# The last chunk of a down projection in two token parts: 192 tokens first, then 128

## The chip, the cores and the metric

The kernel runs on one core of a Trainium2 chip. A core has a matrix engine (TensorE, PE in the profile; PEld is its loading of weights, which stands beside PE), a vector engine (DVE), a scalar engine (ACT), GpSimd (POOL), and SyncE (SP), which here only issues transfers; ACT issues transfers too. Sixteen DMA engines carry the transfers. Matrix products are written to PSUM (eight banks of 128 x 512 float32); everything else lies in SBUF. The metric is the device time of one execution in microseconds (us); lower is better.

## The reference, cut to what matters

One step of a one-layer decoder on 320 tokens (256 of a prompt, 64 of eight running sequences), width 2048. The part that matters here is the last one:

```python
def rms_norm(x, w):
    y = xf * lax.rsqrt(jnp.mean(xf * xf, axis=-1, keepdims=True) + EPS)
    return y * w

f, _ = conv_ffn(rms_norm(x, p["norm_ffn_pre"]), ...)   # ... (gelu(g) * u) @ w_down
x = x + rms_norm(f, p["norm_ffn_post"])                # the output y
```

`w_down` is 5632 x 2048. `f` must be whole for a token, all 2048 columns, before its root (the rsqrt of its mean square) is known; then every column of the token is multiplied by the root, `x` is added, and the result is stored.

## The kernel before, in words

Activations lie with the model dimension on the partitions: `acc[:, nb, :]` is block `nb` (128 of 2048 columns) of `f` for 320 tokens, 16 blocks in all. Every weight is read as float32 and split into two float32r parts, `hi` (ACT casts, L128) and `lo` (DVE subtracts, L130); the activations are split alike (`fhi`, `flo`). One product of 128 x 128 weights is then three matmul instructions in `accumulate` (L141 to L143), each with the weight block loaded anew and 320 columns streamed. `slab` loads 512 KB of weights at a time (SP queue, L124) into rotating buffers, three each of `wraw`, `whi` and `wlo`.

The feed-forward part goes over 11 chunks `g` of 512 inner columns: `ffn_up(g+1)` makes the next chunk, `chunk_out(..., g, ...)` (L222) multiplies chunk `g` into all 16 blocks: for each block four inner tiles times three matmuls, 12 in all, into one of four PSUM banks of pool `mm`; DVE adds the bank to `acc` (L234). In the last chunk `last(nb)` (L1145) follows each block: the block's square is added to a sum over blocks, `sq4` (ACT squares and POOL adds, L299 and L300; the last three blocks by ACT and DVE, L316 to L325), and ACT multiplies the block by its norm weights (L1148).

Then comes the tail, in an order written out by hand (`behind` and `issue_after` chain instructions on an engine):

- `token_sums` (L282): PE multiplies the squares by a column of ones and so sums them over the partitions; once for `sq4`, once for the last block's square `one`;
- `rsqrt_by_root` (L260): a few vector operations on 128 x 3 values and ACT's square root, whose table was loaded earlier by `root_table`;
- `spread` (L286): PE transposes the root back so that it lies along the tokens, in PSUM (`r4`), and for POOL in SBUF (`r4s`);
- `hand_over` (L1228): PE copies blocks of `x1` (the layer's `x`) into PSUM with an identity matrix, in plain float32, for the additions;
- blocks 0 to 3: DVE multiplies by the root (L1259), PE adds the block to `x1` in PSUM (L1269), ACT copies it out (L1270) and stores it; blocks 4 to 11: DVE multiplies and adds (L1264), SP stores; blocks 12 to 15: POOL multiplies and adds (L1276), SP stores.

The tile framework places waits and orders each engine's queue by priority; `first()` is a high priority. Engines run their queues strictly in that order.

Of the kernel before, what the change touches and what calls it, by code (L numbers as in the profile page):

```python
# [17 lines left out]
P = 128  # L18
# [16 lines left out]
def hybrid_step(  # L35
# [21 lines left out]
    def misc(name):  # L57
        return ms.tile([P, 512], F32, tag="ms", name=name)
# [56 lines left out]

    first_raw = []

    def slab(src):
        n = src.shape[2]
        with tc.high_priority(offset=100000):  # L120
            m = n * src.shape[1]
            raw = wp.tile([P, 1024], F32, tag="wraw", name="wraw", bufs=3) if len(first_raw) < 2 else first_raw.pop(0)
            with turn() if first_raw else nullcontext():
                slab_load.append(sp.dma_start(raw[:, :m].rearrange("p (a n) -> p a n", n=n), src).ins)  # L124
            if first_raw:
                in_turn.append(slab_load[-1])
            hi = wp.tile([P, 1024], F32R, tag="whi", name="whi", bufs=3)
            act.copy(hi[:, :m], raw[:, :m])  # L128
            lo = wp.tile([P, 1024], F32R, tag="wlo", name="wlo", bufs=3)
# [9 lines left out]
    def accumulate(ps, w, xhi, xlo, first, last):  # L139
        whi, wlo = w  # L140
        pe.matmul(ps, whi, xhi, start=first, stop=False)  # L141
        pe.matmul(ps, whi, xlo, start=False, stop=False)  # L142
        newest[0] = pe.matmul(ps, wlo, xhi, start=False, stop=last).ins  # L143
# [75 lines left out]
    acc = None  # L219
    pd_last = []  # L220

    def chunk_out(w, ck, hi, lo, begins, done=None, rate=1):  # L222

        for nb in range(KD):
            if nb % 2 == 0:
                wb = slab(rows_of(w, 4 * ck, 4, P * nb, 256))
            ps = mm.tile([P, 512], F32, tag="mm", name=f"pd_{ck}_{nb}")
            for k in range(4):
                made = accumulate(ps[:, :NT], wb(k, nb % 2), hi[:, k, :], lo[:, k, :], k == 0, k == 3)
            with first():  # L230
                if begins:
                    act.copy(acc[:, nb, :], ps[:, :NT])
                else:
                    dve.tensor_tensor(out=acc[:, nb, :], in0=acc[:, nb, :], in1=ps[:, :NT], op=ALU.add)  # L234
# [24 lines left out]

    def rsqrt_by_root(ps, scale):  # L260

        v, w, r, s = (tp.tile([P, 3], F32, tag=f"rq_{n}", name=f"rs_{n}", bufs=1) for n in "vwrs")
        dve.tensor_scalar(out=v, in0=ps, scalar1=scale, scalar2=EPS, op0=ALU.mult, op1=ALU.add)
# [4 lines left out]
        rsqrt_ins.append(dve.scalar_tensor_tensor(out=r, in0=v, scalar=1.5, in1=r, op0=ALU.add, op1=ALU.mult).ins)  # L268
        return r
# [4 lines left out]
        with tc.issue_after(behind):  # L274
            act.activation(there, ones[:, 0:1], AF.Sqrt)

    def token_sums(sq, ps=None, more=False):

        begins = ps is None
        ps = misc("tsum") if begins else ps  # L280
        for c, o in enumerate((0, P, NT - P)):
            ins = pe.matmul(ps[:, c:c + 1], sq[:, o:o + P], ones[:, 0:1], start=begins and c == 0, stop=not more and c == 2).ins  # L282
        sums_ins.append(ins)
        return ps if more else ps[:, 0:3]

    def spread(r, out=None):  # L286

        ps = misc("spread")
        for c, o in ((2, NT - P), (0, 0), (1, P)):
            spread_ins.append(pe.transpose(ps[:, o:o + P], r[:, c:c + 1].to_broadcast([P, P]), ident).ins)  # L290
        if out is not None:
            act.copy(out, ps[:, :NT])
        return ps[:, :NT]

    def add_square(total, x, begins, adder=pool, place=("sq", 2)):
        if begins:
# [761 lines left out]
    with tc.tile_pool(name="fp", bufs=1) as fp:  # L1058
# [81 lines left out]

        sq4 = fp.tile([P, NT], F32, name="sq4")

        squares, one = squares_of(sq4, True)

        def last(nb):  # L1145
            a = acc[:, nb, :]
            squares(nb)
            act.activation(a, a, AF.Copy, scale=col(prm_at["norm"][2] + nb))  # L1148

        def renewals():  # L1150

# [57 lines left out]
        for g in range(NG):  # L1209
            hi, lo = nxt  # L1210
            if g < NG - 1:
                nxt = ffn_up(g + 1)
            if g == 0:
                acc = fp.tile([P, KD, NT], F32, name="acc_ffn")
            if g == NG - 1:
                finish(grow)
            chunk_out(ffn_w_down, g, hi, lo, g == 0, last if g == NG - 1 else None)

        act.dma_start(o_fconv_p, ptf)


        banks, more = (mm, "mm"), (ms, "ms")
        x1p, behind = {}, {}

        def after(engine):
            return tc.issue_after(behind[engine]) if engine in behind else nullcontext()

        def hand_over(*blocks, where=banks):  # L1228
            for nb in blocks:
                x1p[nb] = where[0].tile([P, 512], F32, tag=where[1], name="x1p")[:, :NT]  # L1230
                with after(pe):
                    behind[pe] = pe.matmul(x1p[nb], ident, x1[:, nb, :], start=True, stop=nb > 3).ins

        def stored(queue, k, n):
            with after(queue):
                behind[queue] = queue.dma_start(o_y[:, k:k + n, :], acc[:, k:k + n, :]).ins

        behind[pe] = pd_last[-1]
        with after(pe):
            sums = token_sums(sq4, more=True)  # L1240
        behind[pe] = sums_ins[-1]
        hand_over(0)
        with after(pe):
            sums = token_sums(one[0], sums)
        r = rsqrt_by_root(sums, 1.0 / D)
        behind[pe] = sums_ins[-1]
        hand_over(4, 5)
        with after(pe):
            r4 = spread(r)
        behind[pe] = spread_ins[-1]  # L1250
        with after(pe):
            r4s = fp.tile([P, NT], F32, name="r4s")
            spread(r, r4s)
        behind[pe] = spread_ins[-1]

        def timed(engine, k, n, root):
            f = acc[:, k:k + n, :]
            with after(engine):
                behind[engine] = engine.tensor_tensor(out=f, in0=f, in1=root.unsqueeze(1).to_broadcast([P, n, NT]), op=ALU.mult).ins  # L1259

        def whole(k, n):
            timed(dve, k, n, r4)
            for nb in range(k, k + n):
                behind[dve] = dve.tensor_tensor(out=acc[:, nb, :], in0=acc[:, nb, :], in1=x1p[nb], op=ALU.add).ins  # L1264
            stored(sp, k, n)

        def by_pe(nb):
            with after(pe):
                behind[pe] = pe.matmul(x1p[nb], ident, acc[:, nb, :], start=False, stop=True).ins  # L1269
            act.copy(acc[:, nb, :], x1p[nb])  # L1270
            stored(act, nb, 1)

        def by_pool(k):
            timed(pool, k, 2, r4s)
            with after(pool):
                behind[pool] = pool.tensor_tensor(out=acc[:, k:k + 2, :], in0=acc[:, k:k + 2, :], in1=x1[:, k:k + 2, :], op=ALU.add).ins  # L1276
            stored(sp, k, 2)

        timed(dve, 0, 1, r4)
        hand_over(1)  # L1280
        by_pe(0)
        whole(4, 2)
        hand_over(6, 7, where=more)
        timed(dve, 1, 1, r4)
        by_pe(1)
        by_pool(12)
        whole(6, 2)
        hand_over(2, 8)
        timed(dve, 2, 1, r4)
        by_pe(2)  # L1290
        hand_over(9, 3)
        timed(dve, 3, 1, r4)
        by_pe(3)
        whole(8, 2)
        by_pool(14)
        hand_over(10, 11)
        whole(10, 1)
        whole(11, 1)


_OUTS = [
# [81 lines left out]
```

## Time and profile before

| | us |
|---|---|
| median of 3 runs | 1778.87 (1778.08 to 1780.75) |
| profiled execution | 1777.68 |
| its span, first to last instruction | 1775.6 |
| PE busy | 1765.8 (99%) |
| last product of the last chunk ends | 1759.58 |
| last vector operation ends | 1772.42 |
| last store is issued | 1772.45 |

The granted clock is full in this execution. The page gives busy times by engine and, for groups of equal instructions, line, tile names, shapes, count, total and mean duration, and what ended the idle time before. The chain of waits is followed back from the last instruction. In a timeline a row is one instruction or a run of equal ones (xN) with its start and length. `PEld` rows are weight loads, `SPq` and `ACTq` rows are transfers issued by that engine.

### The profile page before, as it was taken

The numbers are of one execution on the slowest core, as the hardware profiler recorded it, in microseconds if no ns is written. First come the engines' busy times: TensorE is split into PE (matmuls) and PEld (weight loads), VectorE is DVE, ScalarE is ACT, GpSimd is POOL, SyncE is SP. The second block draws the span as 40 slices with busy tenths as digits, with TensorE's granted clock in tenths as the row PEclk, the third lists the DMA queues.
The fourth block names the chain that finished last, engine by engine and source line by source line (L and its number), as shares of the span: only waits on it lengthen the run. The fifth ranks groups of instructions, "written<-read, shape, count | busy, mean of one in ns | idle before, by whom it ended". The sixth has DMA issues, their size and how long they took to land.

```text
span 1775.6 us, 31255 instructions
## 1 busy us (share of the span) xinstructions
PE 1765.8 (99%) x12234; PEld 1740.7 (98%) x12234; DVE 1186.2 (67%) x2055; ACT 799.4 (45%) x1108; POOL 272.7 (15%) x591
## 2 busy tenths in 40 slices
PE   9999999999999999999999999999999999999998
PEld 8999999999999999999999999999999999999998
DVE  7448854657887778577966666767666575656475
ACT  7344545333545454445645434343434343433335
POOL 1003210000211111012322212021101010101004
PEclk9999999999999999999999999999999999999999
DMA  7455654445664654545566656566564445544543
GB/s 245 143 166 167 191 155 149 151 153 185 227 207 150 201 161 145 157 162 155 161 190 198 207 173 208 181 197 205 180 192 147 153 149 152 156 145 154 151 151 106
DMA packets 228498, 303.04 MB, mean 171 GB/s; under 512 B 19488, under 2 KB 150656, under 8 KB 228160
## 3 DMA queue, kind: packets, MB, share of 16 engines
q1 hardware_dynamic: 216560, 281.27, 51.5%
q10 hardware_dynamic: 10304, 15.30, 2.4%
q0 software_dynamic: 1488, 4.49, 0.8%
q8 instruction: 96, 1.57, 0.4%
q14 instruction: 50, 0.41, 0.1%
HBM read 283.44 MB, written 17.58 MB: 170 GB/s over the span
## 4 chain that ended last, share of the span: by engine, by line
PE 95%; DVE 2%; DMA 1%; ACT 1%; issue 0%; POOL 0%; SPq 0%; DVEq 0%; ACTq 0%
PE ps L141 20%; PE ps L143 20%; PE ps L142 20%; PE pd L141 10%; PE pd L142 10%; PE pd L143 10%; PE y_ps L902 1%; DMA cs<-dacs_d 0%; DVE wlo L130 0%; PE sg L708 0%; PE yo_ps L851 0%; PE up_ps L1197 0%; PE tsum L282 0%; DVE acc_mix L1043 0%; PE vt_ps L597 0%
## 5 line engine op out<-in xcount | busy, mean ns | idle before, releaser
L130 DVE TENSOR_TENSOR wlo<-wraw,whi 128x1024 fp32r<-128x1024 f32 x470 | 584.8, 1245 | 385.6 <-ACT whi L128 380.9
L128 ACT CAST whi<-wraw 128x1024 fp32r<-128x1024 f32 x470 | 492.4, 1048 | 706.5 <-PE ps L142 409.0
L141 PE MATMUL ps<-h_hi,whi 128*128 128x320 f32 x2528 | 783.0, 310 | 2.0 <-ACT whi L128 1.8
L143 PE MATMUL ps<-h_hi,wlo 128*128 128x320 f32 x2528 | 779.2, 309 | 1.0 <-DVE wlo L130 1.0
L142 PE MATMUL ps<-h_lo,whi 128*128 128x320 f32 x2528 | 779.8, 309 | 0.0
L141 PEld LDWEIGHTS ps<-h_hi,whi 128*128 128x128 f32 x2528 | 474.4, 188 | 5.5 <-ACT whi L128 2.6
L143 PEld LDWEIGHTS ps<-h_hi,wlo 128*128 128x128 f32 x2528 | 474.1, 188 | 2.3 <-DVE wlo L130 2.2
L142 PEld LDWEIGHTS ps<-h_lo,whi 128*128 128x128 f32 x2528 | 474.6, 188 | 1.5 <-issue 0.5
L141 PE MATMUL pd<-fhi,whi 128*128 128x320 f32 x704 | 217.3, 309 | 0.0
L143 PE MATMUL pd<-fhi,wlo 128*128 128x320 f32 x704 | 217.3, 309 | 0.0
L142 PE MATMUL pd<-flo,whi 128*128 128x320 f32 x704 | 217.3, 309 | 0.0
L141 PE MATMUL pd<-ohi,whi 128*128 128x320 f32 x448 | 139.1, 311 | 0.0
L142 PE MATMUL pd<-olo,whi 128*128 128x320 f32 x448 | 139.0, 310 | 0.0
L143 PE MATMUL pd<-ohi,wlo 128*128 128x320 f32 x448 | 138.7, 310 | 0.0
L142 PEld LDWEIGHTS pd<-flo,whi 128*128 128x128 f32 x704 | 132.2, 188 | 0.7
L143 PEld LDWEIGHTS pd<-fhi,wlo 128*128 128x128 f32 x704 | 132.2, 188 | 0.0
L141 PEld LDWEIGHTS pd<-fhi,whi 128*128 128x128 f32 x704 | 132.2, 188 | 0.0
L234 DVE TENSOR_TENSOR acc_ffn<-acc_ffn,pd 128x320 f32<-128x320 f32 x160 | 77.2, 483 | 33.3 <-PE pd L143 32.3
L141 PEld LDWEIGHTS pd<-ohi,whi 128*128 128x128 f32 x448 | 84.1, 188 | 0.9 <-issue 0.4
L142 PEld LDWEIGHTS pd<-olo,whi 128*128 128x128 f32 x448 | 84.1, 188 | 0.7 <-issue 0.4
L143 PEld LDWEIGHTS pd<-ohi,wlo 128*128 128x128 f32 x448 | 84.1, 188 | 0.2 <-issue 0.2
L1094 POOL COPY ptf<-pad 128x2 f32<-128x2 f32 x88 | 20.9, 240 | 404.2 <-DVE pad L1082 403.7
(300 smaller groups left out, 1576.0 us busy)
## 6 DMA issues: line engine op xcount, KB each, us to landing
wraw<-in_ffn_w_up SPq DMA_DIRECT2D x176, 512.0 KB, 3.7
wraw<-in_w_in SPq DMA_DIRECT2D x142, 512.0 KB, 3.7
wraw<-in_ffn_w_down SPq DMA_DIRECT2D x88, 512.0 KB, 3.5
wraw<-in_w_out SPq DMA_DIRECT2D x64, 512.0 KB, 3.5
st<-in_state_ssm SPq DMA_DIRECT2D x64, 256.0 KB, 4.3
out_ssm_state_sample<-st ACTq DMA_DIRECT2D x32, 256.0 KB, 2.6
cs<-dacs_d SPq DMA_DIRECT2D x16, 320.0 KB, 4.6
xr<-in_xT SPq DMA_DIRECT2D x4, 640.0 KB, 4.6
```

Of the source, the lines that this page charges most:

```text
L128: act.copy(hi[:, :m], raw[:, :m])
L130: dve.tensor_tensor(out=lo[:, :m], in0=raw[:, :m], in1=hi[:, :m].bitcast(F32), op=ALU.subtract)
L141: pe.matmul(ps, whi, xhi, start=first, stop=False)
L142: pe.matmul(ps, whi, xlo, start=False, stop=False)
L143: newest[0] = pe.matmul(ps, wlo, xhi, start=False, stop=last).ins
L234: dve.tensor_tensor(out=acc[:, nb, :], in0=acc[:, nb, :], in1=ps[:, :NT], op=ALU.add)
L902: pe.matmul(ps[64 * i:64 * i + 64, cols], w(hl), x(hl, m, cpx), tile_position=(0, 64 * i), **flags)
L1094: pool.tensor_copy(ptf[:, k, :], pad[:, 256:258])
```

## The change

The last chunk's blocks 0 to 7 are made as before, for all 320 tokens. Its blocks 8 to 15 are made twice: first all eight for tokens 0 to 191, then all eight for tokens 192 to 319. The four weight slabs of these blocks are kept for both passes: three in the rotating `whi`/`wlo` buffers, the first in the `ohi`/`olo` buffers, which are free by then (`place`). Squares, norm weights and sums go in the same two parts.

While the second pass runs, `between` puts the first part's root into it: after late block 9 PE makes the sums for the 192 tokens (two of 128 columns, at 0 and 64) and DVE the root; in late block 13 PE spreads it (two transposes), ACT copies it for POOL, and DVE begins to multiply the first part's blocks by it (`times_root`), POOL to add `x1` (`plus_x1`). After the last product only the second part's sums, root and spread are left, on one 128-column piece; its 16 blocks go four at a time (128 x 512): blocks 0 to 3 by DVE, PE and ACT, 4 to 11 by DVE with `x1` from PSUM, 12 to 15 by DVE alone. DVE and POOL still have first-part blocks to do in between. The stores become eight: four of 128 x 4 x 192 and four of 128 x 4 x 128.

PE's order at the end is in the changed program: 96 products of 192 columns, 24 of 128, two sums, 36 products of 128, three more, two transposes, 33 products, then sum, `x1` of blocks 0 to 3, sum of `one`, `x1` of 4 to 7, a transpose, `x1` of 8 to 11, and the addition of blocks 0 to 3. DVE's order from late block 12 on: its square's sum, `times_root(0,4)`, block 13's addition and sum, `times_root(4,2)`, block 14's two, block 15's addition and square, `times_root(6,2)`, the root, `times_root(8,2)`, then the late blocks, with `times_root(10,2)` after block 7. POOL has two multiplications and six additions of first-part blocks.

The core of the diff:

```diff
-    def chunk_out(w, ck, hi, lo, begins, done=None, rate=1):
+    EARLY_TOK, LATE_TOK = slice(0, 192), slice(192, NT)
+    def chunk_out(w, ck, hi, lo, begins, done=None, rate=1, parted=0, place=None, between=None):
-        for nb in range(KD):
+        for nb in range(KD - parted):
...
+        kept = []
+        for at in (EARLY_TOK, LATE_TOK) if parted else ():
+            n = at.stop - at.start
+            for nb in range(KD - parted, KD):
+                i = nb - KD + parted
+                if i % 2 == 0 and at is EARLY_TOK:
+                    kept.append(slab(rows_of(w, 4 * ck, 4, P * nb, 256), place if i == 0 else None))
+                ps = mm.tile([P, 512], F32, tag="mm", name=f"pd_{ck}_{nb}")
+                for k in range(4):
+                    made = accumulate(ps[:, :n], kept[i // 2](k, i % 2), hi[:, k, at], lo[:, k, at], k == 0, k == 3)
+                with first():
+                    dve.tensor_tensor(out=acc[:, nb, at], in0=acc[:, nb, at], in1=ps[:, :n], op=ALU.add)
+                done(nb, at)
+                if at is LATE_TOK:
+                    between(i)
...
+        def between(i):
+            if i == 1:
+                with first(), tc.issue_after(newest[0]):
+                    sums = token_sums(sq4, at=(0, 64))
+                with first():
+                    roots["r"] = rsqrt_by_root(sums, 1.0 / D)
+            if i == 4:
+                with first(), tc.issue_after(newest[0]):
+                    roots["by"] = spread(roots["r"], at=((1, 64), (0, 0)))
+                with first():
+                    r4s = fp.tile([P, 192], F32, name="r4s")
+                    act.copy(r4s, roots["by"])
+                times_root(0, 4)
+                combined(pool, 12, 2, EARLY_TOK, ALU.mult, wide(r4s, 2))
+                plus_x1(0, 4)
+                stored(sp, 0, 4, EARLY_TOK)
+                combined(pool, 14, 2, EARLY_TOK, ALU.mult, wide(r4s, 2))
+            if i == 5:
+                behind[dve] = folded[-1]
+                times_root(4, 2)
+                plus_x1(4, 2)
+        chunk_out(ffn_w_down, NG - 1, *nxt, False, last, parted=8, place=place, between=between)
...
+                sums = token_sums(sq4, more=True, at=(192,))
+            hand_over(0)
+            times_root(6, 2)
+                sums = token_sums(one[0], sums, at=(0,))
+                r = rsqrt_by_root(sums, 1.0 / D)
+            hand_over(4)
+            times_root(8, 2)
+                r4 = spread(r, at=((0, 0),), ps=mm.tile([P, 512], F32, tag="mm", name="spread"))
+            hand_over(8)
+            plus_x1(6, 2)
+            stored(sp, 4, 4, EARLY_TOK)
+            plus_x1(12, 4)
+            plus_x1(8, 2)
+            combined(dve, 0, 4, at, ALU.mult, wide(r4, 4))
+                behind[pe] = pe.matmul(by_block(x1p[0]), ident, acc[:, 0:4, at], start=False, stop=True).ins
+            act.copy(acc[:, 0:4, at], by_block(x1p[0]))
+            stored(act, 0, 4, at)
+            combined(dve, 4, 4, at, ALU.mult, wide(r4, 4))
+            combined(dve, 4, 4, at, ALU.add, by_block(x1p[4]))
+            stored(sp, 4, 4, at)
+            stored(sp, 12, 4, EARLY_TOK)
+            times_root(10, 2)
+            plus_x1(10, 2)
+            combined(dve, 8, 4, at, ALU.mult, wide(r4, 4))
+            combined(dve, 8, 4, at, ALU.add, by_block(x1p[8]))
+            stored(sp, 8, 4, at)
+            stored(sp, 8, 4, EARLY_TOK)
+            combined(dve, 12, 4, at, ALU.mult, wide(r4, 4))
+            combined(dve, 12, 4, at, ALU.add, x1[:, 12:16, at])
+            stored(sp, 12, 4, at)
```

More of the change, by code (lines that the diff above doesn't have):

```diff
@@ L116, in hybrid_step, with slab @@
     first_raw = []
[L118 removed]
+    def slab(src, place=None):
         n = src.shape[2]
@@ L275, in root_table, with token_sums, spread @@
             act.activation(there, ones[:, 0:1], AF.Sqrt)
[L277 removed]
+    def token_sums(sq, ps=None, more=False, at=(0, P, NT - P)):
         begins = ps is None
         ps = misc("tsum") if begins else ps
[L281 to L282 removed]
+        for c, o in enumerate(at):
+            ins = pe.matmul(ps[:, c:c + 1], sq[:, o:o + P], ones[:, 0:1], start=begins and c == 0,
+                            stop=not more and c == len(at) - 1).ins
         sums_ins.append(ins)
[L284 to L289, printed above, removed]
+        return ps if more else ps[:, 0:len(at)]
+    def spread(r, out=None, at=((2, NT - P), (0, 0), (1, P)), ps=None):
+        ps = misc("spread") if ps is None else ps
+        for c, o in at:
             spread_ins.append(pe.transpose(ps[:, o:o + P], r[:, c:c + 1].to_broadcast([P, P]), ident).ins)
+        n = max(o for _, o in at) + P
         if out is not None:
[L292 to L293 removed]
+            act.copy(out, ps[:, :n])
+        return ps[:, :n]
     def add_square(total, x, begins, adder=pool, place=("sq", 2)):
@@ L1141, in hybrid_step, with squared, last @@
         sq4 = fp.tile([P, NT], F32, name="sq4")
[L1143 to L1148, printed above, removed]
+        one, folded = [], []
+        def squared(nb, at):
+            x, total, n = acc[:, nb, at], sq4[:, at], at.stop - at.start
+            if nb == 0:
+                act.activation(total, x, AF.Square)
+            elif nb < KD - 3 - (at is LATE_TOK):
+                sq = tp.tile([P, NT], F32, tag="sq", name="sq", bufs=2)[:, :n]
+                made = act.activation(sq, x, AF.Square).ins
+                pool.tensor_tensor(out=total, in0=total, in1=sq, op=ALU.add)
+                if nb == KD - 4 and at is EARLY_TOK:
+                    root_table(made)
+            elif nb < KD - 1:
+                sq = misc("sq_ps")[:, :n]
+                act.activation(sq, x, AF.Square)
+                folded.append(dve.tensor_tensor(out=total, in0=total, in1=sq, op=ALU.add).ins)
+            else:
+                one.append(tp.tile([P, NT], F32, tag="sq", name="sq", bufs=2)[:, :n])
+                folded.append(dve.tensor_tensor(out=one[-1], in0=x, in1=x, op=ALU.mult).ins)
+                if at is EARLY_TOK:
+                    dve.tensor_tensor(out=total, in0=total, in1=one.pop(), op=ALU.add)
+        def last(nb, at=slice(0, NT)):
+            with first() if at.start else nullcontext():
+                squared(nb, at)
+                act.activation(acc[:, nb, at], acc[:, nb, at], AF.Copy, scale=col(prm_at["norm"][2] + nb))
         def renewals():
@@ L1214, in hybrid_step @@
                 acc = fp.tile([P, KD, NT], F32, name="acc_ffn")
-            if g == NG - 1:
-                finish(grow)
-            chunk_out(ffn_w_down, g, hi, lo, g == 0, last if g == NG - 1 else None)
+            if g < NG - 1:
+                chunk_out(ffn_w_down, g, hi, lo, g == 0)
         act.dma_start(o_fconv_p, ptf)
-        banks, more = (mm, "mm"), (ms, "ms")
-        x1p, behind = {}, {}
+        finish(grow)
+        behind = {}
         def after(engine):
             return tc.issue_after(behind[engine]) if engine in behind else nullcontext()
[L1228 to L1232, printed above, removed]
@@ L1250, in hybrid_step @@
[L1250 to L1265, printed above, removed]
@@ L1267, in by_pe @@
-        def by_pe(nb):
-            with after(pe):
[L1269 to L1298, printed above, removed]
+        def stored(queue, k, n, at):
+            with after(queue):
+                behind[queue] = queue.dma_start(o_y[:, k:k + n, at], acc[:, k:k + n, at]).ins
@@ new lines, in combined, with wide, times_root, plus_x1 @@
+        def combined(engine, k, n, at, op, other):
+            f = acc[:, k:k + n, at]
+            with after(engine):
+                behind[engine] = engine.tensor_tensor(out=f, in0=f, in1=other, op=op).ins
+        def wide(root, n):
+            return root.unsqueeze(1).to_broadcast([P, n, root.shape[1]])
+        roots = {}
+        def times_root(k, n):
+            combined(dve, k, n, EARLY_TOK, ALU.mult, wide(roots["by"], n))
+        def plus_x1(k, n):
+            combined(pool, k, n, EARLY_TOK, ALU.add, x1[:, k:k + n, EARLY_TOK])
@@ new lines, in hybrid_step, with hand_over, by_block @@
+        place = [hp.tile([P, 4, NT], F32R, tag=tag, name=tag).rearrange("p k n -> p (k n)") for tag in ("ohi", "olo")]
+        chunk_out(ffn_w_down, NG - 1, *nxt, False, last, parted=8, place=place, between=between)
+        at = LATE_TOK
+        x1p = {}
+        def hand_over(k):
+            x1p[k] = mm.tile([P, 512], F32, tag="mm", name="x1p")
+            with after(pe):
+                behind[pe] = pe.matmul(by_block(x1p[k]), ident, x1[:, k:k + 4, at], start=True, stop=k > 0).ins
+        def by_block(ps):
+            return ps.rearrange("p (k n) -> p k n", n=P)
```

28 lines of the change are left out of this document (12 added, 16 removed).

## The prediction, made before the changed kernel ran

> **What bounds the kernel now.** I read the page first, then the chain of waits, then the timeline of the last 16 us.
>
> ```profile
> span 1775.6 us, 31255 instructions
> PE 1765.8 (99%) x12234; PEld 1740.7 (98%) x12234; DVE 1186.2 (67%) x2055; ACT 799.4 (45%) x1108; POOL 272.7 (15%) x591
> PE 95%; DVE 2%; DMA 1%; ACT 1%; issue 0%; POOL 0%; SPq 0%; DVEq 0%; ACTq 0%
> ```
>
> PE is busy throughout and carries 95% of the chain. Two things can therefore move the time: PE's work up to the last product, and the tail behind it.
>
> The chain of waits over the last block (start, length, what):
>
> ```profile
> 1757.82 0.15 PE pd L141
> ...
> 1759.43 0.15 PE pd L143
> 1759.58 0.74 PE tsum L282 x6
> ...
> 1762.71 0.50 PE spread L290 x3
> ...
> 1763.24 1.23 DVE acc_ffn L1259 x2
> ...
> 1768.75 1.08 PE x1p L1232 x4
> ...
> 1771.93 0.49 DVE acc_ffn L1264
> ```
>
> One block is 12 products; from the first to the last are 11 steps, (1759.43-1757.82)/11 = 0.146 us each, without a gap. Call the end of the last product E: 1759.58. From there to the span's end, 1775.6, are 16.0 us. The timeline of that tail:
>
> ```profile
> 1759.62 0.49 DVE L234 TENSOR_TENSOR acc_ffn<-acc_ffn,pd 128x320 f32<-128x320 f32 x1 [0.18 <-PE pd L143]
> 1761.57 0.16 DVE L263 TENSOR_SCALAR rs_v<-tsum 128x3 f32<-128x3 f32 x1 [0.94 <-PE tsum L282]
> 1762.44 0.16 DVE L268 SCALAR_TENSOR_TENSOR rs_r<-rs_v,rs_r 128x3 f32<-128x3 f32 x1
> 1765.40 7.38 SPq L1236 DMA_DIRECT2D out_y<-acc_ffn  x7
> ```
>
> Addition, sums, root and spread take until 1763.24 (3.7 us), multiplying and adding 16 blocks until 1772.42 (9.2 us), the last store until 1775.6 (3.2 us). The change removes about two fifths of the middle part from the tail and pays in PE.
>
> **PE before E: narrower products.** Before, the eight blocks are 96 products of 320 columns: 96 x 0.1464 = 14.05 us. Now they are 96 of 192 and 96 of 128, the same columns, but each weight block is loaded twice. What a load costs shows where it isn't hidden:
>
> ```profile
> 820.15 0.19 PEld L141 LDWEIGHTS ps<-h_hi,whi 128*128 128x128 f32 x1 [0.41 <-ACT h_hi L368]
> 820.16 0.41 PE L141 MATMUL ps<-h_hi,whi 128*128 128x320 f32 x1
> ```
> ```profile
> L141 PE MATMUL ps<-h_hi,whi 128*128 128x320 f32 x2528 | 783.0, 310 | 2.0 <-ACT whi L128 1.8
> L1197 PE MATMUL up_ps<-xsp,kept 128*128 128x512 f32 x32 | 12.6, 393 | 0.0
> ```
> ```profile
> 260.58 0.30 PEld L709 LDWEIGHTS sg<-wS,vt 128*128 128x128 f32 x2
> 260.80 0.53 PEld L708 LDWEIGHTS sg<-wT,vt 128*128 128x128 f32 x4
> 261.25 0.30 PEld L709 LDWEIGHTS sg<-wS,vt 128*128 128x128 f32 x2
> ...
> 1759.49 0.74 PEld L282 LDWEIGHTS tsum<-ones,sq 128*128 128x128 f32 x6 [0.17 <-DVE sq L323]
> ```
>
> The first product after a pause, with its float32r load starting beside it, takes 410 ns against a mean of 310: the load holds it up by 100 ns. In `sg`, plain float32 with 128 and 64 columns, six loads start within 261.25-260.58 = 0.67 us, 112 ns apart, although some feed only 64 columns; for sums of one column they are (0.74-0.19)/5 = 110 ns apart. So loads of 128x128 go one after another, one per 110 to 112 ns, however short the product. At 320 columns, 146 ns, that hides. By columns alone a product of 192 would come every 91 ns and one of 128 every 63: 146 less 128 or 192 times 0.43 ns, from (393-310)/192. Both are below 112, so I take 112 for both.
>
> No row has a float32r product below 320 columns, so this is bounded. Below: width alone, 91+63 = 154 ns a pair against 146, +0.7 us for 96 pairs. Above: if narrow ones cost what plain float32 does, two passes each, 112 ns a pass at 128 columns and, between that and 270 at 320 (four passes in 1.08 us, L1232), some 165 at 192: 554 ns a pair, +39 us. Taken: 192 x 0.112 = 21.5, **+7.45 us**, since the load's 100 ns is measured on the very form. By the Trainium skill (TensorE: Matmul & The Clock Gate, Back-to-back issue gap) pairs of load and product go at about 81 ns at 128 columns; the 110 to 112 here contradict that for 4-byte weights. By that figure the sum below would be 3.0 us less.
>
> Into the second pass come two sums of plain float32, two passes each (six records for three columns above): 4 x 0.112 = 0.45 us, and two transposes. L290's three take 0.50, so 0.2. **+0.65.** I expect no waits of PE: DVE's addition of a narrow block is about 0.3 us, ACT's square and weighting about 0.8, POOL's sum about 0.7, against 12 x 0.112 = 1.34 us a block (rows below, scaled by width), and four banks of slack; up to +1 if one is late. The slab in `ohi` only comes sooner, hidden. E moves by **+8.1** to 1767.7.
>
> **The tail behind E.** Durations by width:
>
> ```profile
> L1100 DVE TENSOR_TENSOR a<-ucv,gcv 128x256 f32<-128x256 f32 x4 | 1.7, 416 | 0.0
> L1101 DVE TENSOR_TENSOR a<-ucv,gcv 128x64 f32<-128x64 f32 x4 | 0.9, 218 | 0.0
> L1259 DVE TENSOR_TENSOR acc_ffn<-acc_ffn,spread 128x640 f32<-128x640 f32 x3 | 2.4, 815 | 0.0
> ```
> ```profile
> L1148 ACT ACTIVATE acc_ffn<-acc_ffn,prm 128x320 f32<-128x320 f32 x16 | 8.9, 562 | 1.5 <-DVE sq L325 1.2
> L299 ACT ACTIVATE sq<-acc_ffn 128x320 f32<-128x320 f32 x12 | 5.6, 469 | 4.1 <-DVE acc_ffn L234 4.1
> ```
> ```profile
> L300 POOL TENSOR_TENSOR sq<-sq,sq 128x320 f32<-128x320 f32 x12 | 13.2, 1098 | 38.8 <-ACT sq L299 38.7
> L1276 POOL TENSOR_TENSOR acc_ffn<-acc_ffn,acc_mix 128x640 f32<-128x640 f32 x2 | 3.1, 1548 | 0.2
> ```
>
> DVE: 0.15 us and 1.04 ns a column, so 0.28 for 128, 0.55 for 384, 0.68 for 512, 0.95 for 768; in a row, not depending on each other, some 0.08 less. POOL: 2.4 ns a column at most: 0.95 for 384, 1.85 for 768. Now DVE's order, in us from E. `times_root(0,4)` can't start before ACT's copy of the spread root, about E-2.8, and holds block 13's addition until E-1.8; `times_root(4,2)` does the same to block 14. So block 15's addition ends at E+0.75 where before it would be E+0.3, its square at 1.1. PE has `x1` of blocks 0 to 3 in hand (512 columns, two passes of 0.27 x 1.6 = 0.43) and makes the last sum by 2.0; the root takes 1.03 as before (1761.57 to 1762.60): 3.05; `times_root(8,2)` fills the wait for the spread: 3.6. Then: two multiplications and an addition to 5.6, when blocks 4 to 7 go to the store; `times_root(10,2)`, multiplication, addition to 7.4, blocks 8 to 11; two more to 8.7. POOL's eight operations sum to 9.3 us from E-2.8, with waits for DVE to E+7.1, just ahead of it. Without a queue for the stores the end is 8.7 + 3.2 + 0.4 (a larger last store) = E+12.3.
>
> But the stores queue. Transfers in the old tail, and in a stretch of almost only 512-byte packets:
>
> ```profile
> DMA  0000000000000000599408999993999999910000
> q1 hardware_dynamic: 1008, 1.97, 30.5%
> ```
> ```profile
> DMA packets 3992, 2.03 MB, mean 203 GB/s; under 512 B 58, under 2 KB 3991, under 8 KB 3991
> q1 hardware_dynamic: 3991, 2.01, 70.1%
> ```
>
> The first, 1759 to 1776 in slices of 0.425 us, shows the engines full while stores last; packets begin about 0.9 us after the first issue (1765.40 for SP, 0.3 before it for ACT) and end about 1.5 us before the span. Its packets, mostly 2560 bytes, run at 1.97 MB/(0.305 x 272 us) = 23.7 bytes per ns and engine; the 504-byte mean of the second (10 us) at 0.701 x 160 us/3991 = 28 ns each, 18. The new stores are 512 packets each, of 512 bytes late (28 ns, 0.90 us over 16 engines) and 768 early (some 38 ns, 1.22 us). Early blocks 0 to 7 go by E+4. From E+5.6 on the other six stores, four late and two early, come faster than they drain: 4 x 0.90 + 2 x 1.22 = 6.0 us. End: 5.6 + 0.9 + 6.0 + 1.5 = **E+14.0**, against 16.0 before: -2.0.
>
> **Sum:** +7.45 + 0.65 - 2.0 = **+6.1 us**. Against the profiled execution, 1777.68, that is 1783.8; it lies 1.2 below the median of the runs, 1778.87, and from that it is 1785.0. I say **1784.5**. If the stores don't queue: -3.7, so +4.4; with loads at 107 and no queue +3.4; with a late engine holding PE and a longer tail +9.
>
> **The rivals.** What a run can tell from no change is some 0.2%, 3.6 us: 1775.3 to 1782.4.
>
> *Loads stay hidden, so no slowdown.* Place: the 192 narrow products; price: +0.7 instead of +7.45. Late blocks then come every 0.8 us, DVE's extra multiplications are bunched behind E and the tail is about 1.3 us longer: +0.7 + 0.65 - 0.7 = +0.7, 1779.5; without a queue of stores -1.0, 1778. It decides below 99 ns a narrow product ((146+51)/2, where 51 x 96 = 3.6 + 2.0 - 0.65). For it: the load row is a first load after a pause. Against: 110 to 112 in every dense row.
>
> *Loads half hidden, no change that can be told.* If a load overlaps the one before it in part, narrow products come midway between width and load: 102 ns at 192 columns, 88 at 128; 190 - 146 = 44 ns a pair, +4.2, and +4.2 + 0.65 - 2.0 = +2.9, 1781.8. Against it: the even 110 to 112 of `sg` and the sums. The skill's 81 ns, named above, would lie near this; no row does.
>
> *Narrow products priced like plain float32:* +39 + 0.65 - 2 = +37.6, 1816.5. The records mark float32r and float32 alike, which leaves it open; the 310 and 393 ns of the two widths show no step.
>
> *The early work isn't off the tail:* POOL, at its slower pace under DVE (mean 1098 ns for 320 columns in L300, 3.4 a column), ends at E+11 and not 7; the two last SP stores wait behind it: E+15.5, +7.6, 1786.5. Part of the range.
>
> **How the numbers follow.** Forecast 0.73, with the fourth rival in it; of that 0.11 lies below 1782.4. Hidden loads 0.12, of which 0.03 faster by over 0.2%. Half hidden: 0.06. Float32 price 0.05. Left over 0.04 for a tail shorter than any I work out: faster. That makes slower 0.62 + 0.05 and a little of the half-hidden: 0.69; faster 0.07; no change 0.24. Range 1778.0 to 1789.0: from the hidden loads to forecast and late engine together. The forecast's own range is 1782 to 1788.
>
> **What would show it.** In the changed profile: narrow products 110 to 112 ns apart at both widths, weight loads without a gap from late in the chunk; E at 1767 to 1768; sums and transposes between products without PE waiting; `times_root(0,4)` ahead of block 13's addition; the last vector operation near E+8.7; DMA engines full from about E+6.5 to the end, the last store's packets well behind its issue. It is wrong if products come at 60 to 95 ns, at 220 or more, or if the tail is under 12 us.

## The result, and the profile after

| | before | after | difference |
|---|---|---|---|
| median of 4 runs, us | 1778.56 (1778.08 to 1780.75) | 1786.85 (1786.33 to 1787.06) | +8.3 |
| ratio, with its 95% interval | | 1.0046 (1.0033 to 1.0058) | |
| span of the profiled execution | 1775.6 | 1784.6 | +9.0 |
| last product of the last chunk ends (E) | 1759.58 | 1768.59 | +9.0 |
| from there to the span's end | 16.0 | 16.0 | 0.0 |

The kernel became slower by 0.46%; forecast were +6.1 us and 1784.5. In the profiled executions the whole shift lies ahead of E, and the tail that was to become 2 us shorter did not.

The first lines of the page after: instructions of each engine, and, last, the shares of the chain by engine.

```profile
span 1784.6 us, 31421 instructions
PE 1768.8 (99%) x12299; PEld 1744.1 (98%) x12299; DVE 1189.6 (67%) x2068; ACT 801.6 (45%) x1121; POOL 277.8 (16%) x599
PE 95%; DVE 3%; DMA 1%; ACT 1%; issue 0%; POOL 0%; SPq 0%; DVEq 0%; ACTq 0%
```

PE is busy for 3.0 us more and still carries 95% of the chain; vector work has gained one percent of it. E is 9.0 us later, so the place to read is the section ahead of it, not PE's total.

**Ahead of E.** PE's rows in the timeline of the kernel after (start, length, engine and line, operation): the last product of 320 columns and the first four of 192, the last three of 128, and the first sum behind them.

```profile
1746.26 0.31 PE L142 MATMUL pd<-fhi,wlo 128*128 128x320 f32 x1
1746.41 0.25 PE L140 MATMUL pd<-fhi,ohi 128*128 128x192 f32 x1
1746.49 0.27 PE L141 MATMUL pd<-flo,ohi 128*128 128x192 f32 x1
1746.61 0.27 PE L142 MATMUL pd<-fhi,olo 128*128 128x192 f32 x1
1746.72 0.28 PE L140 MATMUL pd<-fhi,ohi 128*128 128x192 f32 x1
...
1768.09 0.28 PE L140 MATMUL pd<-fhi,whi 128*128 128x128 f32 x1
1768.21 0.27 PE L141 MATMUL pd<-flo,whi 128*128 128x128 f32 x1
1768.32 0.27 PE L142 MATMUL pd<-fhi,wlo 128*128 128x128 f32 x1
...
1768.84 0.38 PE L298 MATMUL tsum<-ones,sq 128*128 128x1 f32 x2 [0.25 <-DVE sq L1177]
```

Behind the first of them, products start 0.11 to 0.12 us apart at 192 columns and at 128. From the end of the last wide one, 1746.57, to E, 1768.32 + 0.27 = 1768.59, are 22.02 us. The same stretch before:

```profile
1745.19 0.31 PE L143 MATMUL pd<-fhi,wlo 128*128 128x320 f32 x1
...
1759.27 0.31 PE L143 MATMUL pd<-fhi,wlo 128*128 128x320 f32 x1
```

14.08 us, so +7.94. The clock has no part in it: the granted clock is 1.00 in every stretch of both kernels up to E, and the mean over the span, 0.998 after against 1.000 before, is lower by what follows E. The remaining 1.07 us of E's shift were there long before the parted section. The summary of one tile's products early in the feed-forward part (first and last start in the middle), before and after:

```profile
L1197 PE MATMUL up_ps<-xsp,kept x32: 387/393/398, 935.2 to 1326.2; 128*128 128x512 f32 x32
```
```profile
L1236 PE MATMUL up_ps<-xsp,kept x32: 387/393/398, 936.3 to 1327.3; 128*128 128x512 f32 x32
```

Both take 391.0 us from the first to the last; the 1.1 us arose ahead of that, in work that the change doesn't touch. The kernels of the experiments start the same products between 936.0 and 938.3. As they are, the nine starts lie 3.1 us apart; with the distance of each profiled execution from its kernel's median taken off, 1.2 us (936.1 to 937.3, the kernel before at 936.1). So most of it is a difference between executions and not of kernels; what is left of it isn't explained. The prediction said that the profiled execution of before lies 1.2 us under the median; this is the other side of it.

**Behind E.** DVE's rows in the timeline after, from the last block on.

```profile
1768.70 0.28 DVE L252 TENSOR_TENSOR acc_ffn<-acc_ffn,pd 128x128 f32<-128x128 f32 x1
1769.02 0.64 DVE L1180 TENSOR_TENSOR sq<-acc_ffn 128x128 f32<-128x128 f32 x1
1769.58 0.54 DVE L1271 TENSOR_TENSOR acc_ffn<-acc_ffn,spread 128x384 f32<-128x384 f32 x1
1770.34 0.16 DVE L279 TENSOR_SCALAR rs_v<-tsum 128x1 f32<-128x1 f32 x1 [0.22 <-PE tsum L298]
1770.53 0.16 DVE L281 RECIPROCAL rs_w<-rs_v 128x1 f32<-128x1 f32 x1
1770.80 0.68 DVE L282 TENSOR_TENSOR rs_r<-rs_s,rs_w 128x1 f32<-128x1 f32 x1
1771.51 1.72 DVE L283 SCALAR_TENSOR_TENSOR rs_v<-rs_s,rs_r 128x1 f32<-128x1 f32 x1
1773.27 0.16 DVE L284 SCALAR_TENSOR_TENSOR rs_r<-rs_v,rs_r 128x1 f32<-128x1 f32 x1
...
1778.49 0.69 DVE L1271 TENSOR_TENSOR acc_ffn<-acc_ffn,acc_mix 128x512 f32<-128x512 f32 x1
```

One value per partition, and yet L283 takes 1.72 us and L282 0.68, where L284 takes 0.16. The root runs from 1770.34 to 1773.43: 3.1 us, where 1.03 was forecast. POOL's rows of the same time:

```profile
1768.51 0.99 POOL L1271 TENSOR_TENSOR acc_ffn<-acc_ffn,r4s 128x384 f32<-128x384 f32 x1
1769.47 3.75 POOL L1271 TENSOR_TENSOR acc_ffn<-acc_ffn,acc_mix 128x384 f32<-128x384 f32 x3
1773.97 0.99 POOL L1271 TENSOR_TENSOR acc_ffn<-acc_ffn,acc_mix 128x384 f32<-128x384 f32 x1 [0.75 <-DVE acc_ffn L1271]
```

POOL's three additions (`plus_x1` of blocks 4 and 5, of 6 and 7, of 12 to 15) end at 1773.22, and L283 at 1773.23. L282 ends at 1771.48, by which the second of the three is over: the two short ones take 0.99 each, as the row of 1773.97 does, so 1771.45. The square L1180 ends at 1769.66, with 0.64 us instead of the 0.28 of an addition of its width; POOL's multiplication ends at 1769.50. All three have both operands in SBUF. The reading is a hold by POOL, which no row calls a wait: it stands inside the instruction's length. The experiments test it.

The hold has a second effect, on PE. PE waits 2.22 us for the root, and the granted clock, 1.00 until then, is 0.50 from 1774 to 1776: a copy of `x1` for four blocks (two passes of 512 columns) takes 1.92 us, where it took 1.10 ahead of the wait. On DVE this costs little: its three multiplications behind the root take 1.94 us, against 1.78 in the experiment that removes the hold.

### The profile page after: what moved, and what is told of

It is laid out like the page before. It is cut to its first block, busy times and chain, and to the rows that moved or that the text cites. A ratio compares the mean times of both kernels' runs of the same rounds, so it can differ in the third digit from the quotient of the medians.

```text
span 1784.6 us, 31421 instructions
## 1 busy us (share of the span) xinstructions
PE 1768.8 (99%) x12299; PEld 1744.1 (98%) x12299; DVE 1189.6 (67%) x2068; ACT 801.6 (45%) x1121; POOL 277.8 (16%) x599
## 4 chain that ended last, share of the span: by engine, by line
PE 95%; DVE 3%; DMA 1%; ACT 1%; issue 0%; POOL 0%; SPq 0%; ACTq 0%; DVEq 0%
PE ps L140 20%; PE ps L142 20%; PE ps L141 20%; PE pd L140 10%; PE pd L141 10%; PE pd L142 10%; PE y_ps L920 1%; DVE wlo L129 1%; DMA cs<-dacs_d 1%; PE sg L726 0%; DVE acc_mix L1061 0%; PE yo_ps L869 0%; PE up_ps L1236 0%; PE tsum L298 0%; DVE acc_mix L1062 0%
## 5 line engine op out<-in xcount | busy, mean ns | idle before, releaser
L140 PE MATMUL pd<-fhi,whi 128*128 128x320 f32 (+2 forms) x720 | 220.7, 307 | 0.0
L142 PE MATMUL pd<-fhi,wlo 128*128 128x320 f32 (+2 forms) x720 | 220.6, 306 | 0.0
L141 PE MATMUL pd<-flo,whi 128*128 128x320 f32 (+2 forms) x720 | 220.6, 306 | 0.0
L235 DVE TENSOR_TENSOR acc_ffn<-acc_ffn,pd 128x320 f32<-128x320 f32 x152 | 73.4, 483 | 28.9 <-PE pd L142 27.8
```

## The experiments

Each was measured beside the kernel before on the same chip; its medians were 1779.17 (the first four experiments), 1779.06 (`e5_two_stores_less` and `e6_four_blocks_parted`) and 1778.85 (`e7_no_two_sbuf_on_path`). "Difference" is against that.

| | difference, us | ratio (95%) | E to span's end, us |
|---|---|---|---|
| the changed kernel | +8.3 | 1.0046 (1.0033 to 1.0058) | 16.0 |
| e1_root_in_psum | +5.1 | 1.0029 (1.0018 to 1.0040) | 13.9 |
| e2_two_parts_only | +6.9 | 1.0039 (1.0024 to 1.0053) | 16.1 |
| e3_parts_256_64 | +7.6 | 1.0042 (1.0027 to 1.0057) | 16.1 |
| e4_fewer_pool_additions (leaves out work) | +5.4 | 1.0028 (1.0018 to 1.0039) | 13.9 |
| e5_two_stores_less (leaves out work) | +5.7 | 1.0032 (1.0020 to 1.0044) | 14.4 |
| e6_four_blocks_parted | +3.9 | 1.0023 (1.0014 to 1.0033) | 15.6 |
| e7_no_two_sbuf_on_path | +4.2 | 1.0026 (1.0015 to 1.0037) | 15.3 |

**The price of the parts alone.** The kernel before, with nothing but the products of its last eight blocks cut in two, in one bank:

```diff
-            for k in range(4):
-                made = accumulate(ps[:, :NT], wb(k, nb % 2), hi[:, k, :], lo[:, k, :], k == 0, k == 3)
+            for at in (slice(0, 192), slice(192, NT)) if w is ffn_w_down and ck == NF // 4 - 1 and nb >= KD - 8 else (slice(0, NT),):
+                for k in range(4):
+                    made = accumulate(ps[:, at], wb(k, nb % 2), hi[:, k, at], lo[:, k, at], k == 0, k == 3)
```

> The kernel before; the last eight blocks of the last chunk are multiplied in two passes of 192 and 128 columns into the same bank, one block after another; additions, root and tail as before. Theory A (weight loads follow one another every 112 ns and a narrow product waits for its load): 192 narrow products take 21.5 us instead of 14.05, +7.4, nothing given back: 1786.0. Theory B (price by columns): +0.7, 1779.3. Theory C (narrow products as plain float32): +39, 1817.

PE's rows of its timeline, last wide product and last narrow one:

```profile
1747.53 0.31 PE L143 MATMUL pd<-fhi,wlo 128*128 128x320 f32 x1
...
1768.95 0.27 PE L143 MATMUL pd<-fhi,wlo 128*128 128x128 f32 x1
```

1769.22 less 1747.84 is 21.38 us; less 14.08 that is +7.30, against +7.45 in the prediction. The medians differ by 6.9. The two sums and two transposes are the rest of the section: 22.02 less 21.38 is 0.64, against +0.65. So PE's loss is these two terms, and the tail gave none of it back.

**Other widths.** The same edit with 256 and 64 columns tells a price by load from a price by width: by columns alone a pair would cost what one product of 320 does, plus little.

```diff
+            for at in (slice(0, 256), slice(256, NT)) if w is ffn_w_down and ck == NF // 4 - 1 and nb >= KD - 8 else (slice(0, NT),):
```

> As the run with two parts only, with 256 and 64 columns instead of 192 and 128. Theory A (a floor of 112 ns per weight load): 256 columns lie above the floor, 118 ns by width, 64 columns at 112: 230 ns a pair against 146, +8.1, 1786.7. Theory B (a price that falls with the columns, width plus some 49 ns as seen at 128 columns): 118 + 85 = 203, +5.5, 1784.1.

```profile
1746.03 0.31 PE L143 MATMUL pd<-fhi,wlo 128*128 128x320 f32 x1
...
1747.24 0.28 PE L141 MATMUL pd<-fhi,whi 128*128 128x256 f32 x1
1747.36 0.28 PE L142 MATMUL pd<-flo,whi 128*128 128x256 f32 x1
...
1767.95 0.28 PE L142 MATMUL pd<-flo,whi 128*128 128x64 f32 x1
1768.06 0.28 PE L143 MATMUL pd<-fhi,wlo 128*128 128x64 f32 x1
```

256 columns come every 0.12 us (by the prediction's slope of 0.43 ns a column, 146 less 64 times that is 118 ns), 64 columns every 0.11 to 0.12, as 128 and 192 do. The section, from 1746.34 to 1768.34, takes 22.0 us, +7.9, where a floor forecast +8.1 and a price that falls with the columns +5.5. A product of this form, loaded anew, costs the larger of some 112 ns and its columns. That the 112 ns are the load's is argued, from the loads in the sums of one column, and not shown apart: every kernel here has as many loads as products, so no run has such a narrow product without a load of its own.

**The hold by POOL.** If two operands in SBUF are what makes DVE wait, the root is rid of it when one of them lies in PSUM, with POOL's work unchanged:

```diff
-    def rsqrt_by_root(ps, scale):
+    def rsqrt_by_root(ps, scale, psum=False):
...
+        t = v
+        if psum:
+            scratch = misc("rs_ps")
+            s, t = scratch[:, 0:n], scratch[:, 8:8 + n]
...
-        dve.scalar_tensor_tensor(out=v, in0=s, scalar=-0.5, in1=r, op0=ALU.mult, op1=ALU.mult)
-        rsqrt_ins.append(dve.scalar_tensor_tensor(out=r, in0=v, scalar=1.5, in1=r, op0=ALU.add, op1=ALU.mult).ins)
+        dve.scalar_tensor_tensor(out=t, in0=s, scalar=-0.5, in1=r, op0=ALU.mult, op1=ALU.mult)
+        rsqrt_ins.append(dve.scalar_tensor_tensor(out=r, in0=t, scalar=1.5, in1=r, op0=ALU.add, op1=ALU.mult).ins)
...
-                r = rsqrt_by_root(sums, 1.0 / D)
+                r = rsqrt_by_root(sums, 1.0 / D, True)
```

> The changed kernel; in both roots of the tail ACT's square root and the second intermediate lie in PSUM instead of SBUF, so that no vector instruction of the root reads two operands from SBUF. POOL's work is as it was. Theory A (a vector instruction with two SBUF operands waits until POOL's running instruction ends): the last root, from its first to its last instruction, falls from 3.1 us to 1.0 to 1.1, none of its instructions is longer than 0.25, POOL's instructions keep their lengths, and the time falls by 2.1, to about 1784.7. Theory B (the long instructions come from something else that ran then, transfers or a late engine): the root stays at 3.1 and the time at 1786.9.

Its timeline, DVE and POOL:

```profile
1768.69 0.64 DVE L1185 TENSOR_TENSOR sq<-acc_ffn 128x128 f32<-128x128 f32 x1
1769.14 5.86 POOL L1276 TENSOR_TENSOR acc_ffn<-acc_ffn,acc_mix 128x384 f32<-128x384 f32 x5
...
1770.02 0.16 DVE L284 TENSOR_SCALAR rs_v<-tsum 128x1 f32<-128x1 f32 x1 [0.22 <-PE tsum L303]
...
1770.47 0.16 DVE L287 TENSOR_TENSOR rs_r<-rs_ps,rs_w 128x1 f32<-128x1 f32 x1
1770.67 0.17 DVE L288 SCALAR_TENSOR_TENSOR rs_ps<-rs_ps,rs_r 128x1 f32<-128x1 f32 x1
1770.87 0.16 DVE L289 SCALAR_TENSOR_TENSOR rs_r<-rs_ps,rs_r 128x1 f32<-128x1 f32 x1
```

POOL works through the root without a pause, and the root takes 1.0 us: 0.16 or 0.17 for each instruction. The square, left with both operands in SBUF, still takes 0.64. E is 1768.26 and the span ends at 1782.2: a tail of 13.9 us. PE, which waits for no held root, keeps the clock of 1.00, and its copy of `x1` behind the root takes 1.02. The difference of the medians fell by 3.2 us; the trace accounts for 2.1 of that, and the two intervals are wide enough for the rest.

The other side: POOL's three additions that ran during the root are left out (these blocks then lack `x1`), and the operands stay where they were.

```diff
             if i == 5:
                 behind[dve] = folded[-1]
                 times_root(4, 2)
-                plus_x1(4, 2)
+                pass
...
             hand_over(8)
-            plus_x1(6, 2)
             stored(sp, 4, 4, EARLY_TOK)
-            plus_x1(12, 4)
             plus_x1(8, 2)
```

> The changed kernel with POOL's additions of x to blocks 4 to 7 and 12 to 15 of tokens 0 to 191 left out (these blocks lack x); nothing of the vector engine's work is changed. Theory A (POOL's running instruction holds the vector engine's two-SBUF-operand instructions): with POOL idle the last root takes 1.0 to 1.1 us instead of 3.1 and the time falls by 2 to 2.5. Theory B (something else): the root stays at 3.1, the time falls by at most 0.5.

```profile
1768.90 1.00 POOL L1271 TENSOR_TENSOR acc_ffn<-acc_ffn,r4s 128x384 f32<-128x384 f32 x1
...
1769.40 0.65 DVE L1180 TENSOR_TENSOR sq<-acc_ffn 128x128 f32<-128x128 f32 x1
...
1771.19 0.16 DVE L282 TENSOR_TENSOR rs_r<-rs_s,rs_w 128x1 f32<-128x1 f32 x1
1771.38 0.16 DVE L283 SCALAR_TENSOR_TENSOR rs_v<-rs_s,rs_r 128x1 f32<-128x1 f32 x1
...
1772.28 0.99 POOL L1271 TENSOR_TENSOR acc_ffn<-acc_ffn,acc_mix 128x384 f32<-128x384 f32 x1 [2.38 <-DVE acc_ffn L1271]
```

The same instructions on the same tiles take 0.16 us once POOL is idle, and the square, during which POOL's multiplication still runs, keeps its 0.65. The root takes 1.0 us, and from E, 1768.98, to the span's end are 13.9 us, as in the other experiment. Either side alone removes the hold, so it takes both: two operands in SBUF on DVE, and POOL in an instruction of its own. That is shown.

**The stores.** The prediction had the end set by the six late stores, not by the last vector operation. Two stores less, so that their part of the output is not written:

```diff
             stored(sp, 4, 4, at)
-            stored(sp, 12, 4, EARLY_TOK)
...
             stored(sp, 8, 4, at)
-            stored(sp, 8, 4, EARLY_TOK)
```

> The changed kernel without the stores of blocks 8 to 11 and 12 to 15 of tokens 0 to 191 (that part of the output is not written); all else as it was. Theory A (the eight stores come faster than they drain, the last one waits in the queue): 768 KB in packets of 768 bytes less, some 2.4 us of transfer, the last store goes as soon as it is issued; from the end of the last vector operation to the end of the span 3.6 us instead of 5.4, the time 1.8 lower, about 1785. Theory B (the end is the last store's own latency): the 5.4 us stay and the time too.

The DMA engines' busy tenths from 1765 to 1785 in slices of 0.5 us, first of the changed kernel, then of this one:

```profile
DMA  0000000009940019920000009999999999992000
```
```profile
DMA  0000000000299100499000000691089999500000
```

The last vector operation, in the same order:

```profile
1778.49 0.69 DVE L1271 TENSOR_TENSOR acc_ffn<-acc_ffn,acc_mix 128x512 f32<-128x512 f32 x1
```
```profile
1779.18 0.69 DVE L1271 TENSOR_TENSOR acc_ffn<-acc_ffn,acc_mix 128x512 f32<-128x512 f32 x1
```

After the change the engines are full from 1777 to 1783, and the span ends 5.4 us after the last vector operation (1784.6 less 1779.18). Without the two stores there are gaps, and it ends 3.9 us after it (1783.8 less 1779.87): the two stores in the queue are worth 1.5 us of the tail, where 1.8 were expected. In the kernel before, the span ended 3.2 us after the last vector operation.

**Fewer blocks in parts.** With the root repaired as in the first of the POOL experiments, only four blocks are parted, so that PE pays half:

```diff
-            if i == 1:
+            if i == 0:
...
-            if i == 4:
+            if i == 2:
...
-            if i == 5:
+            if i == 3:
...
-        chunk_out(ffn_w_down, NG - 1, *nxt, False, last, parted=8, place=place, between=between)
+        chunk_out(ffn_w_down, NG - 1, *nxt, False, last, parted=4, place=place, between=between)
```

> The changed kernel with the root in PSUM as in the first run, and only the last four blocks in two parts; the early sums come after late block 12, the spread after late block 14. Theory A (price by the number of parted products): 96 narrow products cost 3.7 instead of 7.4, the sums and transposes 0.65 as before; the tail behind the last product 14 us as with eight blocks, or up to 1 longer, since the early work starts at the same distance from the end: 2.3 to 3.3 over the kernel before, about 1781.5. Theory B (the second part needs its eight blocks to cover the early root): PE or the vector engine waits, the tail is 16 or more and the time at 1783 to 1785.

PE's section takes 11.43 us, from 1755.59 to E at 1767.02, against 7.03 for 48 products of 0.1464: +4.4, as worked out. The tail, however, is 15.6 and not 14 to 15, and the time is +3.9 where 2.3 to 3.3 were expected. PE's last wide and last narrow product, then DVE and POOL in its timeline:

```profile
1755.28 0.31 PE L142 MATMUL pd<-fhi,wlo 128*128 128x320 f32 x1
...
1766.74 0.28 PE L142 MATMUL pd<-fhi,wlo 128*128 128x128 f32 x1
...
1767.84 1.80 POOL L1276 TENSOR_TENSOR acc_ffn<-acc_ffn,acc_mix 128x768 f32<-128x768 f32 x1
1767.99 1.79 DVE L1185 TENSOR_TENSOR sq<-acc_ffn 128x128 f32<-128x128 f32 x1
...
1770.64 0.15 DVE L284 TENSOR_SCALAR rs_v<-tsum 128x1 f32<-128x1 f32 x1
```

The early work has come closer to E (POOL's first multiplication starts at E-0.2, in the changed kernel at E-2.9), and a longer addition of POOL falls on the square: 1.79 us, where an addition of its width takes 0.28. The root begins at E+3.6, where it was E+1.75 in the changed kernel. I had repaired the root and left the same form of instruction ahead of it.

**No such instruction ahead of the root.** On top of the last kernel, the late square goes to ACT, and PE's first copy of `x1` behind the last sum; DVE's order is then tied to its additions instead of its squares:

```diff
-                folded.append(dve.tensor_tensor(out=one[-1], in0=x, in1=x, op=ALU.mult).ins)
+                if at is EARLY_TOK:
+                    folded.append(dve.tensor_tensor(out=one[-1], in0=x, in1=x, op=ALU.mult).ins)
+                else:
+                    act.activation(one[-1], x, AF.Square)
...
-            hand_over(0)
...
             behind[pe] = sums_ins[-1]
+            hand_over(0)
             hand_over(4)
```

> As the run with four blocks in two parts, but the square of the last late block is made by ACT, not by the vector engine from twice the same SBUF operand, and the copy of x of blocks 0 to 3 follows the last sum on PE. Theory A (the vector engine's square, 1.79 us in that run, waited for POOL's running addition): the root's first instruction comes 1.3 to 1.7 us sooner behind the last product, the tail falls from 15.6 to about 14.1 us and the time by 1.5, to about 2.3 over the kernel before. Theory B (the square was late for another reason): the tail stays at 15.6. Either way it is not faster than the kernel before, since 4.4 us in PE stand against 1.9 in the tail.

```profile
1767.53 0.16 DVE L284 TENSOR_SCALAR rs_v<-tsum 128x1 f32<-128x1 f32 x1
...
1769.26 5.63 POOL L1279 TENSOR_TENSOR acc_ffn<-acc_ffn,acc_mix 128x384 f32<-128x384 f32 x5
1769.46 1.29 DVE L1279 TENSOR_TENSOR acc_ffn<-acc_ffn,spread 128x512 f32<-128x512 f32 x2 [0.46 <-PE spread L312]
...
1773.95 1.48 DVE L1279 TENSOR_TENSOR acc_ffn<-acc_ffn,acc_mix 128x512 f32<-128x512 f32 x1
```
```profile
DMA  0000000039900069999999999999920000000000
```

E is at 1765.71, so the root begins at E+1.8, 1.8 us sooner than in the kernel before it: that step is right. The time is not: +4.2 against +3.9, no gain that can be told, where 1.5 us were expected. Three things took it. The copies of `x1` that were moved behind the last sum keep PE until 1769.15, and DVE waits 0.46 us for the spread. The last addition, with `x` from SBUF, now runs while POOL adds, and takes 1.48 instead of 0.69 (it ends at 1775.43, POOL at 1774.89). Together that is 1.25 us of the 1.8. And seven stores now follow one another without a gap: the DMA engines are full from 1772 to 1779.5. By the prediction's prices, three early ones of 1.22 and four late of 0.90, that is 7.3 us of transfer, which an earlier root doesn't shorten. The span ends 5.6 us after the last vector operation.

No kernel of these is faster than the one before. The best two, four blocks in parts, lose 4.4 us on PE and win at most 0.7 at the end.

## Why the prediction was right, and where it was not

**Narrow products: right.** Forecast +7.45 from "loads of 128x128 go one after another, one per 110 to 112 ns, however short the product"; alone they cost +7.30. Both ends of that step's bounds, +0.7 by columns and +39 by two passes, are refuted by the rows at 192, 128 and 64 columns. The step of the prediction that carried it was to read the pace of loads where nothing hides it, in sums of one column, and not where it is hidden. By the Trainium skill (TensorE: Matmul & The Clock Gate, Back-to-back issue gap) 128 columns would have gone at 81 ns; the trace has 112 for these four-byte weights, so the measurement decides.

**Sums and transposes in the second pass: right.** They cost 0.64, forecast +0.65; with them the forecast was +8.1, and the section grew by 7.94.

**No waits of PE: right up to E.** The first wait is 0.25 us for block 14's square, just behind E, and the sum of the last square doesn't suffer from it: the root starts at E+1.75, forecast E+2.0. `times_root(0,4)` did hold block 13's addition as said, until 1766.85 (E-1.7; forecast E-1.8), and block 15's addition ended at E+0.4 instead of E+0.75.

**"The root takes 1.03 as before": the step that failed.** It took 3.1 us. The prediction carried the duration over from a place where POOL was idle to one that the change itself had filled with POOL's additions. From the end of the root to the last vector operation it is 5.75 us, forecast 5.65, so everything behind it is the forecast moved by some 1.8 us: the root's 2.07 less the 0.25 that it started sooner. That the tail came out at 16.0 us, as before the change, is chance: what the change saved and what the hold cost happen to be alike. When nothing else is altered than where the root's operands lie, the tail is 13.9, forecast 14.0. In sum +6.1 became +9.0 between the profiled executions: -0.16 from PE, +2.0 from the tail, +1.07 from the difference between executions. Against medians, where that last term should mostly fall away, +7.9 stand beside +8.3 measured.

By the Trainium skill (SBUF — State Buffer, Who interferes with whom) a vector instruction with two inputs in SBUF contends with a GpSimd instruction that reads SBUF; the one that issues second stands still until the first is done, and one with at most one input there, outside the modes that use both ports, does not contend. The trace agrees: 1.72 us, up to the end of POOL's addition, and 0.16 with one operand in PSUM. The prediction had not used this page.

**The stores: right.** The end is set by the queue, not by the last store's issue: with two stores less, 1.5 us went. From the moment that blocks 4 to 7 of the second part are whole (1776.01) to the end are 8.6 us; the forecast's 0.9 + 6.0 + 1.5 is 8.4.

**The rivals.** Hidden and half-hidden loads and the price of plain float32 are excluded by the distances between the products. The rival that came nearest to the time, 1786.5 against 1786.85, has the wrong mechanism: it made POOL late, at E+11. POOL's last addition ended at E+9.0, and it held up vector instructions, not stores.

The forecast was thus of the right sign, with its largest term within 2%; its 1784.5 was 2.4 us low, some 2.0 of it for one term, the shorter tail; the rest is mostly its base, which it set between the profiled execution and the median (1783.8 and 1785.0).

## What to carry to other kernels

A product that streams few columns and loads its weights anew has a floor: with 128 x 128 float32r weights some 112 ns, so that cutting 320 columns in two costs half as much again (21.4 us for 14.1), and an idle engine at the end must be worth more than that. When work is moved beside a chain of tiny vector instructions, ask what else runs on POOL then: an instruction on one value per partition, with two operands in SBUF, waits out the rest of the addition there, and its length hides the wait. Keep one operand of such instructions in PSUM; and before shortening a tail, see whether the stores alone fill it.

## What the runs showed of the hardware that was not expected

- DVE held by POOL: 0.16 us became 0.68 and 1.72 for 128 x 1 elements, and a square of 128 x 128 whose two inputs are the same SBUF tile took 0.64 and 1.79, where an addition of that width takes 0.28. `scalar_tensor_tensor` waits as `tensor_tensor` does. One operand in PSUM: 0.16 and 0.17 while POOL runs on.
- The pace of float32r products, each with its weights loaded anew, has a floor of about 112 ns, the same at 64, 128 and 192 columns; 256 columns take 117 to 120 and 320 take 146.
- Behind a wait of PE of 2.22 us (the changed kernel), and in e6_four_blocks_parted behind two of 1.69 and 0.50 us, the granted clock fell from 1.00 to 0.50, and a copy of `x1` for four blocks took 1.9 us; behind one of 1.22 us (e7_no_two_sbuf_on_path) the clock stayed at 1.00, and the copy took 1.02. How long a wait it takes was not tried.
- A product that stands far ahead of every edit starts between 935.2 and 938.3 us in the profiled executions, a spread of 3.1 us. That is more than a third of the effect studied, so these kernels were told apart by sections of their traces and not by whole spans. A part of it goes with the clock: in four of the nine (e2, e4, e5 and e6) the granted clock was below 1.00 between 800 and 840 us, down to 0.92, and these start the product at 936.7 to 938.3, the other five at 935.2 to 937.0. What makes the rest was not tried.
